# A two-bank score tile and another placement of PSUM banks in the attention stage, and a per-tile end of the down product, in a hybrid decoder block on Trainium2

## The chip, the cores and the metric

The kernel runs on one core of one Trainium2 chip. The metric is device time in microseconds (us), the median of several runs. The profile is one further execution, recorded by the hardware profiler. Engines are named as the profile names them: PE is TensorE (PEld its weight loads), DVE VectorE, ACT ScalarE, POOL GpSimd, SP the queue that issues most DMAs. PSUM, which matmuls write to, is used by this kernel as 8 banks of 512 float32 columns.

## The reference

One decoder block over 1024 tokens of 1024 channels, in float32. The input weight gives a pool branch, queries, keys, values and gates; the attention has 8 query heads on 2 key-value heads of 64 channels, in blocks of 128 queries that see their own and the previous 128 keys, with one sink logit for each head. The MLP is a squared ReLU of width 4096.

```python
def _rmsnorm(x, g):
    xf = x.astype(jnp.float32)
    r = lax.rsqrt(jnp.mean(xf * xf, axis=-1, keepdims=True) + EPS)
    return (xf * r * g.astype(jnp.float32)).astype(x.dtype)
...
    h = _rmsnorm(x, g_mix_pre[l])
    proj = jnp.einsum('bsd,de->bse', h, w_in[l]) + b_in[l]
    u_pool, q, k, v, gates = jnp.split(proj, IN_SPLITS, axis=-1)
...
    y_pool = _multiscale_pool(u_pool, w_pool[l], pool_scale[l])
    q = _partial_rotary(q.reshape(B, S, N_Q_HEADS, HEAD_DIM), cos, sin)
    k = _partial_rotary(k.reshape(B, S, N_KV_HEADS, HEAD_DIM), cos, sin)
...
    y_attn = _sliding_window_sink_attention(
        q.reshape(B, S, N_KV_HEADS, GROUP, HEAD_DIM), k, v, attn_sinks[l])
...
    merged = (g_pool * jnp.einsum('bsc,cd->bsd', y_pool, w_branch_pool[l])
              + g_attn * jnp.einsum('bsc,cd->bsd', y_attn, w_branch_attn[l]))
    mix = jnp.einsum('bsd,de->bse', merged, w_out[l])
    x = x + _rmsnorm(mix, g_mix_post[l])
    h2 = _rmsnorm(x, g_mlp_pre[l])
    ff = jnp.einsum('bsf,fd->bsd',
                    jnp.square(jax.nn.relu(jnp.einsum('bsd,df->bsf', h2, w_up[l]))), w_down[l])
    x = x + _rmsnorm(ff, g_mlp_post[l])
```

## The kernel before

Every float32 operand is split into a high part (a cast on ACT) and the rest (a subtraction on DVE), by `split` (L98, L99), and each product is made of three passes (`PASSES`): high by high, high by low, low by high. One matmul of 512 columns starts about 0.23 us after the one before it. The program is written once in its logical order; a scheduler then orders the instructions of each engine, by readiness and by the tile buffers that are free, and each engine runs its own list strictly in order.

The stages follow one another on TensorE: queries, keys and values of the first four tiles of 128 tokens (the loop over `k` from L162, with `mm_q` L147 and `mm_kv` L153); the attention stage, where the remaining four tiles' products (`qkv_tile`) and later the pool branch's input products (`pool_u`, through `mm_fm`, L345 and L347) are put between the attention's own short matmuls; the pool mixing (`pool_mix`, L524); the gates, the branch products, the output product and the up and down products of the MLP. Gates, up and down go by Strassen's seven products over two-by-two blocks (class `Pairs`, matmuls at L408, for gates and up; L1015 for down).

In the attention stage `post_qkv(n)` transposes queries and keys of tile n into two PSUM banks (L239, L240) and splits them. `score(n, g)` forms the scores of four heads of a tile, 128 queries by 256 keys each. Heads come in pairs, one on each key-value head; the two halves of 64 channels lie on partitions 0 to 63 and 64 to 127 of the same operands, and each half writes a bank of its own. For each of 16 groups (n, g) twelve matmuls (L268) fill two banks, four DVE reductions (L275) add the mask, scale, copy the scores to SBUF and give the row maxima. `attend(n, g)` follows: exponentials with their sums on ACT (L287, L290), the denominator (L292, L293) and the multiplication (L294) on DVE, eight transposes (L300), their splits, twelve matmuls with the values (L307) and a copy (L310). Tile 0 has only its own 128 keys.

The PSUM pool `ps` has two rings of four banks, "at" and "mm". In the attention stage "at" serves the transposed queries and keys, the scores (two banks each time), the transposed weights and the attention's outputs; "mm" serves the query, key and value products and `pool_u`.

`mean_sq` (L706) gives one root mean square for `out_post` and `out_norm`: two Squares with sums on ACT, an addition on DVE, then `rsqrt` (L101): a square root on ACT and five short DVE operations, one of them a Newton step.

The down product runs seven block products of 8 steps each, 24 matmuls for each step, in the order 1, 5, 2, 3, 6, 7, 4. Operands are loaded two steps ahead (`operands`), the blocks of the down weight stay in SBUF in 24 slots of the pool `rp`. The last product (4) ends in tile order: its last `LATE` steps are done for tile after tile, 6 matmuls for each step and tile. Then come the addition to the accumulated block (L1079), the Square and the gain (`fin_half`, L1021, L1022), and `finish` (L1026 on): the sum of the two halves, `rsqrt`, a load of the residual row (L1030), two fused multiply-adds (L1033) and two output transfers. For the last product these are called as

```python
for n0, n1 in ((), ((4, 6),), ((6, 7),), ((7, 8),))[t]:
    finish(n0, n1, (u, v))
```

Of the kernel before, what the change touches and what calls it, by code (L numbers as in the profile page):

```python
# [50 lines left out]
def block_kernel(ctx: ExitStack, tc, xt, x, consts, vecs, sinks, b_qkv, g_post, g_mlp, g_mlp_post,  # L51
# [9 lines left out]
    ps = ctx.enter_context(tc.tile_pool(name="ps", bufs=4, space=bass.MemoryType.PSUM))  # L61
# [23 lines left out]
    def bank(tag, shape=None):  # L85
        return ps.tile([P] + (shape or [512]), F32, tag=tag, name=nm(tag))
# [14 lines left out]
    def rsqrt(out_r, sums, n):  # L101
# [4 lines left out]
        dve.tensor_scalar(ms[:, :n], sums, 1.0 / D, EPS, ALU.mult, ALU.add)  # L106
        r = small()
# [49 lines left out]
    bq = {0: bank("at"), 1: bank("at"), 2: bank("mm"), 3: bank("mm")}  # L157
    bkv = {0: bank("at", [2, 256]), 2: bank("mm", [2, 256])}
# [75 lines left out]
    def post_qkv(n):  # L234
        tf = tfs.pop(n)
        t = tf[:, :768].rearrange("p (h d) -> p h d", d=HD)
        bt, bk = bank("at"), bank("at")
# [15 lines left out]
    def score(n, g):  # L253
# [8 lines left out]
        sb = [bank("at", [2, 256]) for _ in range(2)]  # L262
        for i in range(2):
            m = 2 * g + i
            for j, (qx, kx) in enumerate(((0, khi), (0, klo), (1, khi))):
                for kv in range(2):
                    r = slice(kv * HD, (kv + 1) * HD)
                    pe.matmul(sb[kv][:, i, :nk], qt[r, qx, m * P:(m + 1) * P], kx[r, k0:k0 + nk],  # L268
                              start=j == 0, stop=j == 2)

        for i in range(2):
            for kv in range(2):
                j = 2 * i + kv
                h = 4 * g + j
                dve.tensor_tensor_reduce(s4[:, j, :nk], sb[kv][:, i, :nk], msk, -HD ** -0.5, nsnk[:, h:h + 1],  # L275
# [205 lines left out]
    def pool_u(gi):  # L481
        whi, wlo = load_w(w_u[gi], [NK, P])
        bs = [bank("mm"), bank("mm")]
        mm_fm(bs, whi, wlo, xr, NK)
        u = ga_.tile([P, S], F32, tag="ga", name=nm("u"))
        for th in range(2):
            sl = slice(th * 512, (th + 1) * 512)
            dve.tensor_tensor(u[:, sl], bs[th], rb[:, sl], ALU.mult)
# [51 lines left out]
    ap_pool.__exit__(None, None, None)  # L540
    gp_pool = tc.tile_pool(name="gp", bufs=17, reuse_waits="tile")
# [164 lines left out]
    def mean_sq(src_halves, junk_halves):  # L706
        a = small(2, "sq")
        for i in range(2):
            act.activation(junk_halves[i], src_halves[i], AF.Square, accum_out=a[:, i:i + 1])
        dve.tensor_tensor(a[:, 0:1], a[:, 0:1], a[:, 1:2], ALU.add)  # L710
        r = small(1, "rr")
        rsqrt(r, a[:, 0:1], 1)
# [250 lines left out]
    res = {}  # L963
# [54 lines left out]

    def fin_half(n, dj, v):

        act.activation(junk, v, AF.Square, accum_out=sq[:, dj, n:n + 1])  # L1021
        dve.tensor_tensor(v, v, gfin_b[:, dj * 512:(dj + 1) * 512], ALU.mult)  # L1022
# [22 lines left out]
    for j, (i, s_) in enumerate(steps):  # L1045
# [37 lines left out]
        if i == 6:  # L1083
            finish(0, 4, (c11, c12))
# [71 lines left out]
```

## Time and profile before

| | before |
|---|---|
| median of 3 runs | 1163.75 us (1163.31 to 1164.55) |
| the profiled execution | 1163.43 us |
| its span, first to last instruction | 1161.6 us |
| mean granted TensorE clock | 0.996 |
| last value product of attention (L307) starts | 172.63 |
| last of the pool branch's input products (L347) starts | 195.1 |
| last output on VectorE (L1033) ends | 1158.01 |

Times inside the profile count from the start of the span. A matmul's busy time is from its start to its modelled end, and successive ones overlap, so rates are read from starts. "PE at L268 x12" in the chain of waits is a stretch of twelve instructions of TensorE on tiles of the ring "at" from line 268.

### The profile page before, as it was taken

What the parts mean: (1) busy time and instruction counts of PE and PEld (TensorE: products, weight loads), DVE (VectorE), ACT (ScalarE), POOL (GpSimd) and SP (SyncE); (2) the same over time, 40 slices, a digit from 0 to 9 for tenths busy, and PEclk for the clock granted to TensorE, in tenths of its full rate; (3) what the DMA queues carried; (4) which work ended last, traced back from release to release, by engine and by line L of the source; (5) the groups of instructions that cost most, each with busy time, mean ns of one, the idle gap of its engine ahead of it and who ended that gap; (6) DMA issues with size and microseconds to landing.
All of it is one profiled execution on the core that took longest, in us unless ns stands there. A gap on an engine that the chain in (4) does not pass through costs nothing.

```text
span 1161.6 us, 14370 instructions
## 1 busy us (share of the span) xinstructions
PE 1137.1 (98%) x5356; PEld 941.3 (81%) x5356; DVE 827.4 (71%) x1337; ACT 533.8 (46%) x926; POOL 53.5 (5%) x66
## 2 busy tenths in 40 slices
PE   7999999999999999999999999999999999999995
PEld 6888888788888887888788888888888888888884
DVE  7767899888754585777998766667558945447795
ACT  6445655653332233464655453535344345344341
POOL 3411100000000050000000000000000000000000
PEclk9999999999999999999999999999999999999998
DMA  7202114545245453333266434353788564332852
GB/s 257 66 1 91 38 55 163 200 172 172 110 174 189 145 199 109 127 128 127 91 217 217 171 128 181 118 181 118 285 294 295 202 194 133 91 104 77 273 181 91
DMA packets 66167, 179.11 MB, mean 154 GB/s; under 512 B 6192, under 2 KB 6192, under 8 KB 66096
## 3 DMA queue, kind: packets, MB, share of 16 engines
q1 hardware_dynamic: 60480, 157.99, 40.3%
q10 hardware_dynamic: 5616, 20.19, 4.5%
q8 instruction: 42, 0.69, 0.3%
q14 instruction: 29, 0.24, 0.1%
HBM read 127.82 MB, written 50.33 MB: 153 GB/s over the span
## 4 chain that ended last, share of the span: by engine, by line
PE 91%; DVE 4%; ACT 2%; DMA 2%; issue 1%; SPq 0%; DVEq 0%; ACTq 0%
PE mm L408 21%; PE at L408 16%; PE at L1015 15%; PE mm L1015 11%; PE mm L345 8%; PE mm L732 5%; PE mm L347 4%; PE mm L147 3%; PE at L307 2%; PE at L268 2%; PE mm L153 1%; PE at L147 1%; PE at L300 1%; DMA st<-in_w_up_dram 1%; DVE T L99 1%
## 5 line engine op out<-in xcount | busy, mean ns | idle before, releaser
L1015 PE MATMUL at<-ar,wh 128*128 128x512 f32 x744 | 169.3, 389 | 0.0
L1015 PEld LDWEIGHTS at<-ar,wh 128*128 128x128 f32 x744 | 139.6, 188 | 29.0
L1015 PE MATMUL mm<-ar,wh 128*128 128x512 f32 x576 | 131.0, 389 | 0.0
L99 DVE TENSOR_TENSOR wh<-raw,wh 128x1024 fp32r<-128x1024 f32 x53 | 64.8, 1224 | 86.4 <-ACT wh L98 86.4
L1015 PEld LDWEIGHTS mm<-ar,wh 128*128 128x128 f32 x576 | 108.1, 188 | 22.5
L98 ACT CAST wh<-st 128x512 fp32r<-128x512 f32 (+1 forms) x106 | 67.0, 641 | 119.6 <-PE mm L408 36.9
L98 ACT CAST wh<-raw 128x1024 fp32r<-128x1024 f32 x53 | 55.8, 1053 | 134.5 <-PE at L1015 63.4
L99 DVE TENSOR_TENSOR wh<-st,wh 128x512 fp32r<-128x512 f32 (+1 forms) x106 | 82.9, 790 | 18.3 <-ACT wh L98 16.1
L408 PE MATMUL mm<-gr,wh 128*128 128x512 f32 x300 | 72.4, 391 | 0.1
L408 PE MATMUL mm<-T,wx 128*128 128x512 f32 x288 | 67.6, 389 | 0.0
L408 PEld LDWEIGHTS mm<-gr,wh 128*128 128x128 f32 x300 | 56.0, 188 | 12.0 <-ACT g L797 0.5
L408 PEld LDWEIGHTS mm<-T,wx 128*128 128x128 f32 x288 | 54.1, 188 | 11.2
L408 PE MATMUL at<-T,wx 128*128 128x512 f32 x252 | 59.1, 389 | 0.0
L408 PEld LDWEIGHTS at<-T,wx 128*128 128x128 f32 x252 | 47.3, 188 | 9.8
L408 PE MATMUL mm<-x,wh 128*128 128x512 f32 x216 | 51.5, 390 | 0.9 <-ACT g L415 0.9
L99 DVE TENSOR_TENSOR ar<-B,ar 128x1024 fp32r<-128x1024 f32 x37 | 45.1, 1220 | 7.3 <-ACT ar L98 7.3
L408 PEld LDWEIGHTS mm<-x,wh 128*128 128x128 f32 x216 | 40.4, 188 | 10.1 <-ACT g L415 1.7
L408 PE MATMUL at<-gr,wh 128*128 128x512 f32 x183 | 44.6, 390 | 0.0
L290 ACT ACTIVATE s<-s,nmx 128x256 f32<-128x256 f32 (+1 forms) x64 | 31.3, 493 | 26.5 <-DVE nmx L275 26.4
L98 ACT CAST ar<-B 128x1024 fp32r<-128x1024 f32 x37 | 38.9, 1050 | 9.0 <-DMA B<-in_w_dn_dram 4.7
L408 PEld LDWEIGHTS at<-gr,wh 128*128 128x128 f32 x183 | 34.3, 188 | 7.6 <-DVE wh L99 0.4
L650 DVE TENSOR_TENSOR g<-g,mm 128x512 f32<-128x512 f32 x32 | 20.6, 683 | 27.7 <-PE mm L347 27.6
(332 smaller groups left out, 2292.8 us busy)
## 6 DMA issues: line engine op xcount, KB each, us to landing
raw<-f_dram SPq DMA_DIRECT2D x53, 512.0 KB, 3.7
f_dram<-g SPq DMA_DIRECT2D x30, 512.0 KB, 3.3
B<-in_w_dn_dram SPq DMA_DIRECT2D x24, 512.0 KB, 6.3
st<-in_w_up_dram SPq DMA_DIRECT2D x22, 512.0 KB, 3.7
f_dram<-g ACTq DMA_DIRECT2D x17, 512.0 KB, 2.6
st<-in_w_g_dram SPq DMA_DIRECT2D x16, 512.0 KB, 3.7
g<-spill_dram SPq DMA_DIRECT2D x16, 512.0 KB, 4.4
raw<-in_w_dn_dram SPq DMA_DIRECT2D x16, 512.0 KB, 4.6
```

The source lines that it names most:

```text
L98: act.copy(hi, src)
L99: eng.tensor_tensor(lo, src, f32(hi), ALU.subtract)
L147: pe.matmul(bq, xs_[k][n // 4][:, xh, n % 4 * P:(n % 4 + 1) * P], wq[k][:, h, :], start=k == 0 and j == 0, stop=k == NK - 1 and j == 2)
L268: pe.matmul(sb[kv][:, i, :nk], qt[r, qx, m * P:(m + 1) * P], kx[r, k0:k0 + nk], start=j == 0, stop=j == 2)
L290: act.activation(s4[:, j, :nk], s4[:, j, :nk], AF.Exp, scale=-1.0, bias=nmx[:, h:h + 1], accum_out=den[:, h:h + 1])
L307: pe.matmul(yb.rearrange("p m q -> p (m q)"), vs[k0 // P + kb][:, vh, kv * HD:kv * HD + P], pts[kv][:, ph, kb, :], start=j == 0, stop=j == ...
L345: pe.matmul(bs[th], whi[:, k, :], rhs(k, hl, th), start=k == 0 and hl == 0, stop=False)
L347: pe.matmul(bs[th], wlo[:, k, :], rhs(k, 0, th), start=False, stop=k == nk - 1)
L408: pe.matmul(b, w[:, wh, kt, :], xo[kt][:, xh, :], start=not after and kt == 0 and j == 0, stop=kt == 3 and j == 2, skip_group_check=after)
L650: dve.tensor_tensor(z[:, sl], z[:, sl], bs[th], ALU.mult)
L732: pe.matmul(obs[n][dj], l, wos[k][whl][:, dj * 512:(dj + 1) * 512], start=k == 0 and hl == 0 and whl == 0, stop=k == NK - 1 and hl == 1)
L1015: pe.matmul(bs[t], fo[fh][:, k2, t * P:(t + 1) * P], wo_[wh][:, k2, :], start=not after and s2 == 0 and k2 == 0 and j == 0, stop=s2 == NS ...
```

## The change

In the attention stage a pool `psa` replaces `ps`: one tile "sc" of two banks, and rings of three banks "at" and "mm". Both halves of a score group go into the one "sc" tile, so they get their banks together; their matmuls have high priority, and the order of the passes is changed. The first query products use the "sc" tile and "mm", the first key and value products "at". `post_qkv` takes its banks from "mm" for tiles 2 to 7. `pool_u` makes its two halves of 512 tokens one after the other, each with a bank of its own. After `pool_in(0)` the old `ps` with its two rings of four is opened, with waits by tile.

`mean_sq` and the end use a new `rsqrt_sum`: the Squares are scaled by D to the power of -1/2, epsilon is added to one of the two sums ahead of time, and the square root takes the other sum with that as its bias.

In the down product `LATE` is 3; each tile of the last product is finished by itself, its gained half goes into the accumulator `c11`, which is free by then, the residual rows of tiles 4 to 7 are loaded in front into slots of `rp`, the half that is ready earlier (`dj` 1) goes out first, and the last tile's transfer of that half is issued by ACT.

```diff
@@ -58,7 +58,9 @@
     sp = ctx.enter_context(tc.tile_pool(name="sp", bufs=3))
-    ps = ctx.enter_context(tc.tile_pool(name="ps", bufs=4, space=bass.MemoryType.PSUM))
+    psa_pool = tc.tile_pool(name="psa", bufs=1, space=bass.MemoryType.PSUM)
+    psum = {"pool": psa_pool.__enter__(), "bufs": {"sc": 1, "at": 3, "mm": 3}}
@@ -83,7 +85,7 @@
     def bank(tag, shape=None):
-        return ps.tile([P] + (shape or [512]), F32, tag=tag, name=nm(tag))
+        return psum["pool"].tile([P] + (shape or [512]), F32, tag=tag, name=nm(tag), bufs=psum["bufs"][tag])
@@ -115,6 +117,29 @@
+    ROOT_D = D ** -0.5
+    def rsqrt_sum(out_r, a, b, n=1):
+        s = small()
+        ms = small()
+        if n == 1:
+            act.activation(s[:, :1], a, AF.Sqrt, bias=b)
+            dve.tensor_tensor(ms[:, :1], a, b, ALU.add)
+        else:
+            dve.tensor_tensor(ms[:, :n], a, b, ALU.add)
+            act.activation(s[:, :n], ms[:, :n], AF.Sqrt)
+        r = small()
+        dve.reciprocal(r[:, :n], s[:, :n])
+        t = small()
+        if n == 1:
+            dve.scalar_tensor_tensor(t[:, :1], r[:, :1], r[:, :1], ms[:, :1], ALU.mult, ALU.mult)
+        else:
+            dve.tensor_tensor(t[:, :n], r[:, :n], r[:, :n], ALU.mult)
+            dve.tensor_tensor(t[:, :n], t[:, :n], ms[:, :n], ALU.mult)
+        dve.tensor_scalar(t[:, :n], t[:, :n], -0.5, 1.5, ALU.mult, ALU.add)
+        dve.tensor_tensor(out_r, r[:, :n], t[:, :n], ALU.mult)
@@ -154,8 +179,9 @@
-    bq = {0: bank("at"), 1: bank("at"), 2: bank("mm"), 3: bank("mm")}
-    bkv = {0: bank("at", [2, 256]), 2: bank("mm", [2, 256])}
+    bq01 = bank("sc", [2, 512])
+    bq = {0: bq01[:, 0, :], 1: bq01[:, 1, :], 2: bank("mm"), 3: bank("mm")}
+    bkv = {0: bank("at", [2, 256]), 2: bank("at", [2, 256])}
     bss = bank("at", [NT])
@@ -234,7 +260,7 @@
         t = tf[:, :768].rearrange("p (h d) -> p h d", d=HD)
-        bt, bk = bank("at"), bank("at")
+        bt, bk = (bank("at" if n < 2 else "mm") for _ in range(2))
         for m in range(4):
@@ -259,20 +285,22 @@
         nmx = soft[n][0]
-        sb = [bank("at", [2, 256]) for _ in range(2)]
-        for i in range(2):
-            m = 2 * g + i
-            for j, (qx, kx) in enumerate(((0, khi), (0, klo), (1, khi))):
-                for kv in range(2):
-                    r = slice(kv * HD, (kv + 1) * HD)
-                    pe.matmul(sb[kv][:, i, :nk], qt[r, qx, m * P:(m + 1) * P], kx[r, k0:k0 + nk],
-                              start=j == 0, stop=j == 2)
+        sb = bank("sc", [2, 2, 256])
+        with tc.high_priority():
+            for i in range(2):
+                m = 2 * g + i
+                for j, (qx, kx) in enumerate(((0, klo), (1, khi), (0, khi))):
+                    for kv in range(2):
+                        r = slice(kv * HD, (kv + 1) * HD)
+                        pe.matmul(sb[:, kv, i, :nk], qt[r, qx, m * P:(m + 1) * P], kx[r, k0:k0 + nk],
+                                  start=j == 0, stop=j == 2)
...
                 h = 4 * g + j
-                dve.tensor_tensor_reduce(s4[:, j, :nk], sb[kv][:, i, :nk], msk, -HD ** -0.5, nsnk[:, h:h + 1],
+                dve.tensor_tensor_reduce(s4[:, j, :nk], sb[:, kv, i, :nk], msk, -HD ** -0.5, nsnk[:, h:h + 1],
                                          ALU.add, ALU.min, nmx[:, h:h + 1])
@@ -480,12 +508,15 @@
         whi, wlo = load_w(w_u[gi], [NK, P])
-        bs = [bank("mm"), bank("mm")]
-        mm_fm(bs, whi, wlo, xr, NK)
         u = ga_.tile([P, S], F32, tag="ga", name=nm("u"))
...
             sl = slice(th * 512, (th + 1) * 512)
-            dve.tensor_tensor(u[:, sl], bs[th], rb[:, sl], ALU.mult)
+            b = bank("mm")
+            for k in range(NK):
+                for j, (xh, h) in enumerate(PASSES):
+                    pe.matmul(b, (whi, wlo)[h][:, k, :], xr(k, xh, th), start=k == 0 and j == 0,
+                              stop=k == NK - 1 and j == 2)
+            dve.tensor_tensor(u[:, sl], b, rb[:, sl], ALU.mult)
         act.activation(u, u, AF.Identity, bias=vec[:, V_BU + gi:V_BU + gi + 1])
@@ -538,6 +569,10 @@
     ap_pool.__exit__(None, None, None)
+    psa_pool.__exit__(None, None, None)
+    psum["pool"] = ctx.enter_context(tc.tile_pool(name="ps", bufs=4, space=bass.MemoryType.PSUM,
+                                                reuse_waits="tile"))
+    psum["bufs"] = {"at": 4, "mm": 4}
     gp_pool = tc.tile_pool(name="gp", bufs=17, reuse_waits="tile")
@@ -706,10 +741,11 @@
         for i in range(2):
-            act.activation(junk_halves[i], src_halves[i], AF.Square, accum_out=a[:, i:i + 1])
-        dve.tensor_tensor(a[:, 0:1], a[:, 0:1], a[:, 1:2], ALU.add)
+            act.activation(junk_halves[i], src_halves[i], AF.Square, scale=ROOT_D, accum_out=a[:, i:i + 1])
+        b = small()[:, :1]
+        dve.tensor_scalar(b, a[:, 0:1], EPS, None, ALU.add)
         r = small(1, "rr")
-        rsqrt(r, a[:, 0:1], 1)
+        rsqrt_sum(r, a[:, 1:2], b)
         return r
@@ -960,7 +996,7 @@
     junk = dl.tile([P, 512], F32, tag="junk", name="junk", bufs=1)
-    res = {}
+    res, xf = {}, {}
@@ -1016,25 +1052,37 @@
+    def fin_sq(n, dj, v):
+        act.activation(junk, v, AF.Square, scale=ROOT_D, accum_out=sq[:, dj, n:n + 1])
+    def fin_gain(dj, o, v):
+        dve.tensor_tensor(o, v, gfin_b[:, dj * 512:(dj + 1) * 512], ALU.mult)
     def fin_half(n, dj, v):
-        act.activation(junk, v, AF.Square, accum_out=sq[:, dj, n:n + 1])
-        dve.tensor_tensor(v, v, gfin_b[:, dj * 512:(dj + 1) * 512], ALU.mult)
-    def finish(n0, n1, hv):
-        ns = slice(n0, n1)
-        dve.tensor_tensor(sq[:, 0, ns], sq[:, 0, ns], sq[:, 1, ns], ALU.add)
-        rsqrt(rr[:, ns], sq[:, 0, ns], n1 - n0)
-        for n in range(n0, n1):
-            xs = stage([D])
-            nc.sync.dma_start(xs, x1_dram[n])
-            for dj in range(2):
-                o = xs[:, dj * 512:(dj + 1) * 512]
-                dve.scalar_tensor_tensor(o, hv[dj][n % 4], rr[:, n:n + 1], o, ALU.mult, ALU.add)
-                nc.sync.dma_start(out[n][:, dj * 512:(dj + 1) * 512], o)
+        fin_sq(n, dj, v)
+        fin_gain(dj, v, v)
+    def load_x1(n):
+        t = rp.tile([P, 2, 512], F32, tag="w", name=nm("xf"))
+        nc.sync.dma_start(flat(t), x1_dram[n])
+        xf[n] = t
+    def add_eps(ns, dj):
+        dve.tensor_scalar(sq[:, dj, ns], sq[:, dj, ns], EPS, None, ALU.add)
+    def fin_out(n, hv):
+        if n not in xf:
+            t = stage([2, 512])
+            nc.sync.dma_start(flat(t), x1_dram[n])
+            xf[n] = t
+        for dj in (1, 0):
+            o = xf[n][:, dj, :]
+            dve.scalar_tensor_tensor(o, hv[dj][n % 4], rr[:, n:n + 1], o, ALU.mult, ALU.add)
+            (nc.scalar if dj and n == NT - 1 else nc.sync).dma_start(out[n][:, dj * 512:(dj + 1) * 512], o)
     PRODUCTS = (1, 5, 2, 3, 6, 7, 4)
-    LATE = 2
+    LATE = 3
     steps = [(i, s_) for i in PRODUCTS for s_ in range(NS)]
@@ -1075,13 +1123,22 @@
             else:
+                n = 4 + t
                 down_mm(i, s_, bs, False, [(s2, k2, t) for s2 in range(NS - LATE, NS) for k2 in range(2)])
                 dve.tensor_tensor(u[t], u[t], bs[t], ALU.add)
-                fin_half(4 + t, 0, u[t])
-                for n0, n1 in ((), ((4, 6),), ((6, 7),), ((7, 8),))[t]:
-                    finish(n0, n1, (u, v))
+                fin_sq(n, 0, u[t])
+                fin_gain(0, c11[t], u[t])
+                rsqrt_sum(rr[:, n:n + 1], sq[:, 0, n:n + 1], sq[:, 1, n:n + 1])
+                fin_out(n, (c11, v))
+        if i == 7:
+            add_eps(slice(4, NT), 1)
+            for n in range(4, NT):
+                load_x1(n)
         if i == 6:
-            finish(0, 4, (c11, c12))
+            add_eps(slice(0, 4), 1)
+            rsqrt_sum(rr[:, 0:4], sq[:, 0, 0:4], sq[:, 1, 0:4], 4)
+            for n in range(4):
+                fin_out(n, (c11, c12))
     rpool.__exit__(None, None, None)
```

## The prediction

> **What bounds the kernel now.** I read the summary of busy time first, then a table of stretches (start:end, length, busy time and instructions of TensorE, its weight loads, VectorE, ScalarE and GpSimd).
>
> ```profile
> span 1161.6 us, 14370 instructions
> ...
> PE 1137.1 (98%) x5356; PEld 941.3 (81%) x5356; DVE 827.4 (71%) x1337; ACT 533.8 (46%) x926; POOL 53.5 (5%) x66
> ...
> 60.00:108.00 48.00, 48.00 (x332) 41.45 (x332) 31.67 (x86) 24.62 (x75) 8.81 (x15) 1.00 0.08 26
> 108.00:140.00 32.00, 31.52 (x220) 25.98 (x217) 26.41 (x82) 20.74 (x70) 3.83 (x9) 1.00 0.24 79
> 140.00:173.00 33.00, 32.84 (x202) 27.33 (x201) 30.43 (x74) 19.49 (x53) 0.00 (x0) 1.00 0.14 49
> 173.00:196.00 23.00, 23.00 (x106) 19.16 (x105) 21.27 (x36) 11.21 (x16) 0.00 (x0) 1.00 0.45 160
> 196.00:229.00 33.00, 31.89 (x138) 25.43 (x137) 28.17 (x45) 22.31 (x37) 0.00 (x0) 1.00 0.54 184
> ...
> 500.00:545.00 45.00, 44.83 (x205) 36.53 (x204) 31.96 (x78) 24.43 (x64) 0.00 (x0) 1.00 0.41 142
> ```
>
> TensorE works 98% of the span and its clock is full (the 1.00 before the DMA share), so an edit pays only if it takes matmul time away, fills a pause of TensorE, or shortens the end, where TensorE is done. But a busy TensorE is not one at its best rate. In the attention stage the chain of waits (start, length, what) shows the same score work at two prices:
>
> ```profile
> 59.72 0.78 PE at L268 x5
> 61.79 0.78 PE at L268 x6
> ...
> 107.72 0.91 PE at L268 x12
> 108.63 1.02 PE at L300 x8
> ...
> 125.29 0.91 PE at L268 x6
> 126.19 1.50 PE at L307 x11
> 127.69 0.90 PE at L268 x6
> ...
> 145.38 1.32 PE at L307 x11
> ...
> 159.44 0.91 PE at L268 x6
> ...
> 163.01 0.90 PE at L268 x6
> ...
> 172.63 1.30 PE at L307 x11
> ...
> 228.80 1.36 PE at L408 x6
> ```
>
> Twelve score matmuls with the two key-value halves in turn take 0.91 us (107.72): the halves lie on different rows of the array and run side by side. Six of one half alone take 0.91 us too (125.29), and the other six follow later (127.69). This chain shows 8 of the 14 groups of tiles 1 to 7 split so, from 59.72/61.79 to 159.44/163.01: the second half's bank was not free in time, so the order of before puts other work between.
>
> **The change part by part.**
>
> *Scores.* In the order of the changed kernel all 14 groups stand as twelve neighbours with the halves alternating, since both get their banks at once. Eight times 0.90 us: −7.2 us.
>
> *The wait that it adds.* There is one such pair of banks. A group's scores wait until the four reductions (L275) of the group before have read it; behind them on TensorE, which runs in order, wait the transposes, value products and fillers. And the products of the pool branch (L345, L347) have lost their place: the banks of the last tiles' transposes (L239) now come from the ring that the pool branch needs, so only 32 of its 192 matmuls stand inside the attention stage; before, the first stood at 109.4:
>
> ```profile
> L345 PE MATMUL mm<-x,wh x128: 387/389/504, 109.4 to 194.6; 128*128 128x512 f32 x128
> ...
> L347 PE MATMUL mm<-x,wh x64: 387/389/504, 114.0 to 195.1; 128*128 128x512 f32 x64
> ```
>
> So after the last QKV product comes a stretch with 10 groups to be transposed and multiplied with the values, but hardly a filler. Before gets there at 107.72 with 8 score groups left, after with 6. Its start of that stretch: three of the split groups lie ahead of it (−2.7), two score groups more are done (+1.8), and the stage begins worse (+1.7), as the timeline of its start suggests:
>
> ```profile
> 53.28 1.28 ACT L290 ACT_TABLE_LOAD   x1 [0.80 <-DVE nmx L275]
> ...
> 56.35 0.17 DVE L292 TENSOR_TENSOR den<-den,es 128x4 f32<-128x4 f32 x1 [0.98 <-ACT s L290]
> ```
>
> The first exponentials wait for a table load of 1.28 us, and L292 waits for them. The order of after puts this L292 ahead of the reductions that free the pair for the next scores; the 1.7 is an estimate, the load and 0.4 for what queues behind it. 107.72 + 0.8 = 108.5. VectorE's prices, from its timeline further on:
>
> ```profile
> 108.66 0.48 DVE L275 CUSTOM_DVE_ANT_0 s<-at,cst,nsnk 128x256 f32<-128x256 f32 x1
> ...
> 109.88 0.48 DVE L275 CUSTOM_DVE_ANT_0 s<-at,cst,nsnk 128x256 f32<-128x256 f32 x1
> ...
> 110.29 1.29 DVE L99 TENSOR_TENSOR pt<-at,pt 128x512 fp32r<-128x512 f32 x2
> 111.50 0.15 DVE L286 TENSOR_TENSOR es<-snk,nmx 128x4 f32<-128x4 f32 x1
> ...
> 123.50 0.18 DVE L293 RECIPROCAL den<-den 128x4 f32<-128x4 f32 x1
> 123.71 1.22 DVE L294 TENSOR_TENSOR s<-s,den 128x1024 f32<-128x1024 f32 x1
> 124.88 1.29 DVE L99 TENSOR_TENSOR pt<-at,pt 128x512 fp32r<-128x512 f32 x2
> ```
>
> Four reductions take 1.63 us (108.66 to 110.29), the multiplication 1.17 (123.71 to 124.88), the two splits 1.21 (110.29 to 111.50), the three short ones about 0.15 each. Ten groups: 10 × 2.83 + 6 × 1.63 = 38.1 us, and the splits of two tiles' queries and keys, by the row of two splits some 0.8 a tile, 1.6 more: 39.7. TensorE has 10 × (1.02 + 1.32) + 6 × 0.91 + 32 × 0.23 + twelve transposes of these tiles, 1.5 by the row of eight = 37.7. The two are near each other and VectorE is the longer, so the stretch ends near 108.5 + 41 = 149.5, with 1.3 us for hops between engines. The 160 pool matmuls left follow at the rate of the last block (24.64 us for 108, quoted below): 36.5 us, to 186.0. Before, the last of them started at 195.1 and ended its share at 195.3. That is 9.3 us ahead.
>
> *What it gives back.* After the pool branch its split must again come ahead of L524 and of the gate's first products. With the pool work in one block TensorE can wait some 2 us there, where 1.1 stand idle now (196 to 229: 31.89 of 33), so 9.3 − 1 = 8.3 is left. That supposes each engine always has its next instruction ready. In the order of after, a multiplication (L294) often stands among the reductions that free the pair, so some groups come later: I take −7.0. Ends: −9.6, if the hops cost nothing; and if each of the six remaining groups waits for a multiplication (6 × 1.17) and VectorE also carries two splits of pool weights in the stretch, 2.4 us by the same rate, 8.3 − 7.0 − 2.4 = −1.1, a loss of about 1 us.
>
> [...]
>
> *Mean squares.* Epsilon is added beside the second Square and the root is taken right behind it, so one handover from VectorE to ScalarE goes and the count on VectorE stays. The stretch from 500 to 545, where most of them are, has TensorE busy for 44.83 of 45: hidden. −0.2, between 0 and −0.8.
>
> *The end.* Three rather than two steps of the last product are done tile by tile, each tile is finished by itself, and the residual rows are in place beforehand.
>
> ```profile
> 1124.80 24.64 PE L1015 MATMUL at<-ar,wh 128*128 128x512 f32 x108
> ...
> 1132.97 1.05 ACT L98 CAST wh<-raw 128x1024 fp32r<-128x1024 f32 x1 [3.44 <-PE at L1015]
> ...
> 1151.15 0.69 DVE L1022 TENSOR_TENSOR u<-u,bc 128x512 f32<-128x512 f32 x1
> ...
> 1151.83 0.68 DVE L1079 TENSOR_TENSOR u<-u,at 128x512 f32<-128x512 f32 x1
> ...
> 1153.14 0.19 ACT L1021 ACTIVATION_READ_ACCUMULATOR junk<-u 128x1 f32 x1
> ...
> 1155.44 0.29 ACT L104 ACTIVATE sm<-fsq,eps 128x1 f32<-128x1 f32 x1 [2.11 <-DVE fsq L1026]
> ...
> 1155.77 0.16 DVE L108 RECIPROCAL sm<-sm 128x1 f32<-128x1 f32 x1 [0.17 <-ACT sm L104]
> ...
> 1156.60 0.75 DVE L1033 SCALAR_TENSOR_TENSOR st<-u,frr,st 128x512 f32<-128x512 f32 x1
> 1157.27 0.74 DVE L1033 SCALAR_TENSOR_TENSOR st<-v,frr,st 128x512 f32<-128x512 f32 x1
> ```
>
> The last matmul ends at 1124.80 + 24.64 = 1149.44, the last tile's addition starts only at 1151.83, because VectorE is still finishing tiles 4 to 6. The root waits until 1155.44, though its sum is there at 1153.33, behind two outputs and the gain of tiles 6 and 7. After the change a tile costs: addition to sum 1.50 (1151.83 to 1153.33), root 0.35 with its hop, reciprocal to the first output 0.83 (1155.77 to 1156.60), two outputs 0.67 + 0.74: 4.1 us, and VectorE can take the next tile 4.03 after the one before. TensorE delivers the tiles 16, 18 and 18 matmuls apart, 11.86 us by 24.64/108 each, against 3 × 4.03 = 12.09: the last tile starts about 0.2 late. The third late step needs the last operand sooner: its slot comes free at 1132.97 and the operand, two casts and VectorE's splits, is ready about 3.45 us later, while 15 matmuls, 3.41 us, stand ahead of its use: under 0.1 us. So the last output ends at 1149.44 + 0.1 + 0.25 + 4.1 = 1153.9, where it ended at 1158.01: −4.1, and the final transfer, 3.6 us to the end of the span, stays behind it. I take −4.0. Ends: −4.4; and −2.9, if each of the four tiles loses 0.3 us in hops. The residual's loads are issued in product 3 on SP between loads that wait for the same splits, so nothing is held up by them.
>
> *Sum,* in the profiled execution's own time of 1163.43 us (span 1161.6 and 1.8 around it): 1163.43 − 7.0 − 0.2 − 4.0 = 1152.2; the median of the runs shown, 1163.75, is 0.3 above it, so 1152.5.
>
> **The rivals.**
>
> 1. *The pair of banks is the limit.* TensorE's gain in the scores turns whole into waits for the reductions; the stretch of ten groups lasts as long as its fillers did. For it: VectorE's 39.7 us against TensorE's 37.7, and 30.43 of 33 busy on VectorE already. Against it: the fillers' time is not lost, it is done later at full rate. Attention 0 to −2, end and mean squares −4.2: 1163.75 − 5.2 = 1158.5.
>
> 2. *Slower.* The pair comes free late by a multiplication, 1.17 us, for each of the 14 groups, and nothing fills the pause: 16.4 us, with the start's 1.7, against 7.2 + 4.2 gained: +6.7, 1170; it decides from (11.4 − 1.7)/14 = 0.7 us per group on. For it: TensorE runs in order and there is one pair. Against: in the first half the order has QKV products between the groups, and VectorE is busy for 31.67 of 48 there, so only the six late groups have no cover: −11.4 + 1.7 + 6 × 1.17 is still a gain.
>
> 3. *The end does not shorten as told:* the outputs of the last tiles come close together and the final transfer lasts longer, or the late operand stops TensorE by more than 1 us. For it: the slot of 1132.97 is on the edge. Against: the outputs of before were as dense. End 0, the rest −7.2: 1156.5.
>
> 4. *More than forecast:* the sum above holds without the margin, −8.3 to −9.6, with −4.4 and −0.8: 1163.75 − 13.5 to − 14.8, about 1149.5.
>
> **How the numbers follow.** Forecast 0.50, the fourth case 0.13, the first 0.20, the third 0.06, the second 0.11. About 0.2% is what a measurement of this kernel can tell from no change. The range reaches from 1148, under the fourth case with a margin of 1 us, to 1160.5, past the first and third; outside lie the second case and the edges. Slower 0.09, since the second case can also end near no change, same 0.03, faster 0.88. The forecast's own range is 1149.5 to 1156.
>
> **What would show it.** In the profile after: all score groups as runs of twelve in 0.91 us; L345 and L347 mostly after the last value product, which ends near 149, not 174; the first matmul of L408 into "at" near 221, not 228.8; the stage of the up product of equal length; the last tile's addition within 0.5 us of the last matmul, and 12.2 us from that matmul to the end of the span turned into about 8. It is wrong if TensorE shows pauses of a microsecond at most score groups, if the value products still end after 160, or if the last addition still starts 2 us late.

## The result, and the profile after

The changed kernel takes 1156.03 us (median of 4 runs, 1155.0 to 1157.23) against 1163.53 us (4 runs, 1163.2 to 1164.55): a ratio of 0.9933, with a 95% interval of 0.992 to 0.9946. That is 7.5 us less, where 11.3 less was forecast. The profiled execution took 1155.82 us, with a span of 1154.0.

Summary of busy time of the kernel after:

```profile
span 1154.0 us, 14409 instructions
...
PE 1131.8 (98%) x5356; PEld 937.4 (81%) x5356; DVE 826.6 (72%) x1339; ACT 535.0 (46%) x927; POOL 49.1 (4%) x66
```

Its table of stretches, with the columns of the prediction's:

```profile
60.00:108.00 48.00, 47.05 (x326) 39.19 (x324) 36.30 (x118) 28.07 (x97) 6.05 (x16) 0.96 0.01 2
108.00:140.00 32.00, 30.91 (x249) 26.62 (x250) 30.08 (x87) 24.95 (x79) 3.03 (x8) 1.00 0.34 116
...
196.00:229.00 33.00, 31.41 (x136) 24.72 (x135) 27.15 (x43) 18.61 (x32) 0.00 (x0) 1.00 0.49 172
```

TensorE's busy time fell by 5.3 us (1137.1 to 1131.8), the span by 7.6. Two stretches have lost something: from 60 to 108 TensorE stands idle for 0.95 us, where it had no idle time, and its clock is 0.96; and from 108 to 140 VectorE is busy for 30.08 of 32.

The scores do what the diff says. From the chain of waits after (start, length, what):

```profile
100.84 0.91 PE sc L296 x12
...
154.15 19.96 PE mm L517 x88
```

All groups now stand as one run of about 0.9 us, and the products of the pool branch (L517), but for the first 32, follow the last values as one block. To see where the time came from, milestones are better than shares. These are groups of instructions of the kernel after (count: shortest, median and longest duration in ns, first and last start in us, shape):

```profile
L178 PE MATMUL mm<-wkv,x x96: 274/283/562, 50.5 to 111.5; 128*128 128x256 f32 x96
L335 PE MATMUL at<-pt,v x180: 274/282/415, 61.3 to 153.9; 128*128 128x256 f32 x180
L517 PE MATMUL mm<-x,wh x192: 389/389/482, 127.9 to 191.4; 128*128 128x512 f32 x192
L768 PE MATMUL mm<-wohi,gr x128: 389/389/482, 442.3 to 530.8; 128*128 128x512 f32 x128
L1051 PE MATMUL at<-gr,wh x24: 389/389/389, 841.5 to 846.7; 128*128 128x512 f32 x24
```

and of the kernel before:

```profile
L153 PE MATMUL mm<-wkv,x x144: 277/283/384, 12.8 to 107.4; 128*128 128x256 f32 x144
L307 PE MATMUL at<-pt,v x180: 274/282/388, 59.4 to 173.6; 128*128 128x256 f32 x180
L732 PE MATMUL mm<-wohi,gr x128: 389/389/476, 445.7 to 533.9; 128*128 128x512 f32 x128
L1015 PE MATMUL at<-gr,wh x24: 389/389/389, 844.6 to 849.8; 128*128 128x512 f32 x24
```

The last key and value product starts 4.1 us later than before (111.5 against 107.4), but with three more score groups done. The score matmuls ahead of that point, first before, then after (start:end, length, busy time and instructions of TensorE and of its weight loads):

```profile
50.00:107.50 57.50, 9.46 (x84) 7.34 (x84) 1.00 0.06 18
...
50.00:111.50 61.50, 9.58 (x120) 7.68 (x120) 0.97 0.02 7
```

At twelve for a group these are seven groups and ten. The last value product starts 19.7 earlier, since the pool products now come behind it; the last of those starts 3.7 earlier (191.4 against the 195.1 of L347), and the output product 3.4 earlier, the down product 3.1. So the attention stage gave 3.4 us, where 7.0 were forecast, and 0.3 was lost again between output and down product.

The end, from the timeline of the kernel after (start, length, engine, line, operation):

```profile
1123.68 22.88 PE L1051 MATMUL at<-ar,wh 128*128 128x512 f32 x99
...
1142.73 0.68 DVE L1128 TENSOR_TENSOR u<-u,at 128x512 f32<-128x512 f32 x1
...
1146.70 0.68 DVE L1128 TENSOR_TENSOR u<-u,at 128x512 f32<-128x512 f32 x1
...
1150.00 0.74 DVE L1081 SCALAR_TENSOR_TENSOR xf<-c,frr,xf 128x512 f32<-128x512 f32 x1
```

The last matmul ends at 1123.68 + 22.88 = 1146.56, and the last tile's addition starts 0.14 us later, where it was 2.39 late before. A tile takes VectorE 3.97 us (1142.73 to 1146.70). From the last matmul to the end of the span are 7.4 us instead of 12.2, so the end gave 4.7.

The start of the attention stage cost more than was forecast. First VectorE and then TensorE, from the timeline around it:

```profile
57.09 0.16 DVE L320 TENSOR_TENSOR den<-den,es 128x4 f32<-128x4 f32 x1 [1.93 <-ACT s L318]
...
57.38 0.32 DVE L303 CUSTOM_DVE_ANT_0 s<-sc,cst,nsnk 128x128 f32<-128x128 f32 x1
...
58.68 0.39 PE L296 MATMUL sc<-klo,qt 64*128 64x256 f32 x2 [2.13 <-DVE nmx L303]
```

The table of stretches there:

```profile
56.00:58.00 2.00, 0.55 (x6) 0.31 (x3) 0.87 (x7) 1.25 (x7) 0.00 (x0) 1.00 0.00 0
...
60.00:62.00 2.00, 1.87 (x8) 1.38 (x6) 2.00 (x6) 1.38 (x6) 1.36 (x4) 0.50 0.00 0
62.00:64.00 2.00, 2.00 (x10) 1.82 (x9) 2.00 (x11) 0.38 (x2) 0.00 (x0) 0.65 0.00 0
```

L320 waits 1.93 us for the first exponentials, the four reductions that empty the pair of banks stand behind it on VectorE, and the third group's scores stand behind those: TensorE pauses for 2.13 us. Then its granted clock falls to 0.50 from about 60 on (0.65 over 62 to 64), and the matmuls of that time count as busy while they take twice as long: the key and value product at 60.02 takes 0.56 us, where the median of its group is 0.283. Busy time alone would not have shown it; the clock column does.

### The profile page after: what moved, and what is told of

The parts are those of the page before. It is cut to its first block, busy times and chain, and to the rows that moved or that the text cites. A ratio compares the mean times of both kernels' runs of the same rounds, so it can differ in the third digit from the quotient of the medians.

```text
span 1154.0 us, 14409 instructions
## 1 busy us (share of the span) xinstructions
PE 1131.8 (98%) x5356; PEld 937.4 (81%) x5356; DVE 826.6 (72%) x1339; ACT 535.0 (46%) x927; POOL 49.1 (4%) x66
## 4 chain that ended last, share of the span: by engine, by line
PE 88%; DVE 5%; ACT 4%; DMA 2%; issue 1%; SPq 0%; DVEq 0%; ACTq 0%
PE mm L436 20%; PE at L436 16%; PE at L1051 14%; PE mm L1051 11%; PE mm L768 5%; PE mm L373 5%; PE mm L517 4%; PE mm L172 3%; PE mm L375 2%; PE at L335 2%; PE sc L172 1%; PE at L178 1%; PE sc L296 1%; ACT s L318 1%; PE at L328 1%
## 5 line engine op out<-in xcount | busy, mean ns | idle before, releaser
L436 PE MATMUL mm<-x,wh 128*128 128x512 f32 x216 | 51.4, 391 | 0.5 <-ACT g L443 0.5
L436 PEld LDWEIGHTS mm<-x,wh 128*128 128x128 f32 x216 | 40.3, 188 | 9.7 <-ACT g L443 1.1
L517 PE MATMUL mm<-x,wh 128*128 128x512 f32 x192 | 47.7, 393 | 0.0
L517 PEld LDWEIGHTS mm<-x,wh 128*128 128x128 f32 x192 | 35.4, 188 | 6.5
```

Source lines behind the costliest of these rows:

```text
L436: pe.matmul(b, w[:, wh, kt, :], xo[kt][:, xh, :], start=not after and kt == 0 and j == 0, stop=kt == 3 and j == 2, skip_group_check=after)
L517: pe.matmul(b, (whi, wlo)[h][:, k, :], xr(k, xh, th), start=k == 0 and j == 0, stop=k == NK - 1 and j == 2)
```

## The experiments

Each kernel ran beside the kernel before on the same chip. Each expectation says what the theories it weighs would give.

| Kernel | Median, us | Ratio to before | 95% interval |
|---|---|---|---|
| after | 1156.03 | 0.9933 | 0.992 to 0.9946 |
| end_only | 1160.33 | 0.9962 | 0.995 to 0.9974 |
| late2 | 1156.71 | 0.9934 | 0.9922 to 0.9946 |
| exp_early | 1154.12 | 0.9907 | 0.9893 to 0.992 |
| red_first | 1157.94 | 0.9943 | 0.9932 to 0.9954 |
| score_serial | 1154.77 | 0.9919 | 0.9905 to 0.9933 |
| score_twice | 1170.9 | 1.0065 | 1.0053 to 1.0078 |
| post_at | 1153.08 | 0.9908 | 0.9894 to 0.9922 |
| post_at_exp | 1159.12 | 0.9963 | 0.995 to 0.9976 |
| post_at47_exp | 1157.58 | 0.9947 | 0.9933 to 0.9961 |
| post_at_exp_yt | 1152.45 | 0.9913 | 0.9899 to 0.9926 |
| post_at_yt | 1155.74 | 0.9935 | 0.9922 to 0.9947 |
| best_wide | 1152.48 | 0.9901 | 0.9884 to 0.9919 |

**end_only: the end and the mean squares alone.** The kernel before, with only `rsqrt_sum`, `mean_sq` and the new end of the diff.

```diff
-        rsqrt(r, a[:, 0:1], 1)
+        rsqrt_sum(r, a[:, 1:2], b)
...
-    LATE = 2
+    LATE = 3
```

> The kernel before with only the new end and the new mean square; the attention stage is that of before. By the two traces the last matmul ends 2.9 us earlier after the change and the way from there to the end of the span is 4.7 us shorter (12.16 to 7.45), so theory A (the parts are independent) expects about 1163.5 - 4.7 - 0.2 = 1158.6 us. Theory B (part of the 2.9 us comes from the mean squares in the middle) expects under 1157.5.

By the ratio it is 4.4 us faster than before (0.0038 of 1163.5), which leaves 0.9962 − 0.9933 = 0.0029, or 3.4 us, for the attention part; both ratios are good to about 1.4 us. The traces of after divide it in a like way: 3.4 up to the output product and 4.7 at the end, with 0.5 lost between them. The mean squares lie between the output product and the down product, and there is nothing in it, by groups of this kernel:

```profile
L756 PE MATMUL mm<-wohi,gr x128: 389/389/476, 447.1 to 535.4; 128*128 128x512 f32 x128
...
L1039 PE MATMUL at<-gr,wh x24: 389/389/390, 846.1 to 851.3; 128*128 128x512 f32 x24
```

From the first start of one to the first of the other are 399.0 us, before 398.9.

**late2: two instead of three late steps.**

```diff
-    LATE = 3
+    LATE = 2
```

> The changed kernel with two rather than three steps of the last product in tile order. Theory A: TensorE then delivers a tile each 2.7 us and VectorE takes 4.0 for one, so the last tile starts about 3 x 1.3 = 3.9 us late instead of 0.2, less what the sooner operand saves: 1159 to 1160. Theory B: the finish tile by tile is the whole gain: within 0.5 us of 1156.

The medians can't tell it from after. Its profile can. Timeline:

```profile
1124.73 21.24 PE L1051 MATMUL at<-ar,wh 128*128 128x512 f32 x93
...
1146.79 0.67 DVE L1128 TENSOR_TENSOR u<-u,at 128x512 f32<-128x512 f32 x1
...
1151.38 0.74 DVE L1081 SCALAR_TENSOR_TENSOR xf<-c,frr,xf 128x512 f32<-128x512 f32 x1
```

The last matmul ends at 1145.97, the last addition starts 0.82 later, and the last output ends at 1152.12, 6.15 behind the last matmul; after, it was 1150.74 − 1146.56 = 4.2. So the third late step is worth 2 us behind the last matmul in this execution, less than was expected: VectorE interleaves two tiles here (the third tile's addition starts at 1143.37, between two short operations of the second tile, at 1143.29 and 1143.96), and the 4.0 us that one tile takes in after include waits for ACT (0.17 us ahead of L133) that the next tile's work can fill.

**exp_early: the exponentials' table loaded ahead of the stage.** One small exponential more, behind the root of the input sums.

```diff
     rsqrt(r1, bss[:, :NT], NT)
+    act.activation(warm, r1[:, :1], AF.Exp)
```

> The changed kernel with one exponential of a spare value put behind the first square root, so that the table load of 1.28 us falls before the attention stage. Theory A: the missing gain is lost at the start, where the pair of banks is read late behind the table load, TensorE pauses 2.1 us at 56 and then runs at half clock from 60 to 63.5; without the load the pause shrinks under 1 us, no half clock follows: 2 to 3 us less, 1153 to 1154. Theory B: the loss is spread over all groups by the single pair of banks: at most 1 us less, 1155 to 1156.

It is 0.0026, or 3.0 us, better than after by the ratios and 1.9 by the medians; the two intervals only touch. Its table of stretches:

```profile
56.00:58.00 2.00, 1.08 (x11) 0.84 (x10) 1.27 (x6) 0.63 (x5) 0.00 (x0) 1.00 0.00 0
...
60.00:62.00 2.00, 2.00 (x20) 1.86 (x18) 1.66 (x8) 1.37 (x6) 1.65 (x4) 1.00 0.00 0
```

Its key and value products, by groups:

```profile
L178 PE MATMUL mm<-wkv,x x96: 277/283/385, 51.5 to 109.8; 128*128 128x256 f32 x96
```

The pause has shrunk to 0.92 us, the half clock at 60 is gone, and the longest of the products takes 385 ns, not 562. From the first to the last of them are 58.3 us instead of 61.0, so the start cost after 2.7 us. All that this kernel gains is there: from the last of them to the output product are 330.7 us, after 330.8. In this execution it gives back 1.0 us ahead of the stage: the first of these products starts at 51.5, in after at 50.5, behind a half clock from 44 to 48 (0.51, then 0.63) that the trace of after does not have (1.00).

**red_first: the reductions ahead.** The loop of the four reductions stands in `tc.high_priority()`.

```diff
+        with tc.high_priority():
             for i in range(2):
                 for kv in range(2):
```

> The changed kernel with the four reductions of each group at high priority like their matmuls, so that they stand ahead of denominators and multiplications on VectorE and free the pair sooner. Theory A (loss at the start): the reductions of the second group no longer wait for the first exponentials, the pause at 56 goes: 2 to 3 us less, 1153 to 1154. Theory B (the pair is the limit in every group): still more, 3 to 5 us less. Theory C (VectorE's total is the limit): earlier reductions only delay the multiplications: within 1 us of 1156.

It is about 1 us slower than after by the ratios, which the intervals leave open; it is not faster. At the start it did not do what it was for: the denominator still comes first and the pause stays. Later on, the value products wait longer for the casts of the weights. Waits of TensorE from 44 to 210 (engine, what, waited for: us in total, times, longest), first of this kernel, then of after:

```profile
PEld at L336 <- ACT pt L100: 4.7, 14, 0.5
...
PE sc L296 <- DVE nmx L304: 2.1, 1, 2.1
```

```profile
PEld at L335 <- ACT pt L100: 3.0, 9, 0.5
...
PE sc L296 <- DVE nmx L303: 2.1, 1, 2.1
```

In after, the matmuls of the scores wait for the reductions once for more than 0.2 us, the 2.1 us of the start. Past the start, then, the time at which the pair comes free isn't what binds. The waits for the casts grow from 3.0 to 4.7, those for the subtractions fall from 2.8 to 2.2; that the precedence of the reductions is the reason is not shown. This run does not test the start itself.

**score_serial: one half's three matmuls, then the other's.**

```diff
-                for j, (qx, kx) in enumerate(((0, klo), (1, khi), (0, khi))):
-                    for kv in range(2):
-                        r = slice(kv * HD, (kv + 1) * HD)
+                for kv in range(2):
+                    r = slice(kv * HD, (kv + 1) * HD)
+                    for j, (qx, kx) in enumerate(((0, klo), (1, khi), (0, khi))):
```

> The changed kernel with the twelve matmuls of a score group in another order: three of one half, then three of the other, twice, in the same two banks. A group takes then at least 1.4 us by the row of six of one half in 0.91, less up to three overlaps at the changes of half, instead of 0.91. Theory A (score time is on the path, as the forecast supposed): 14 groups x 0.5 to 0.9 = 7 to 12 us more, 1163 to 1168. Theory B (TensorE would only wait longer for VectorE and ScalarE in this stage, so the score time saved turned into waits): 0 to 3 us more, 1156 to 1159.

The time is that of after within the intervals. The order on TensorE is now low, high, high for one half and then the same for the other, but its timeline shows one group so:

```profile
139.76 0.39 PE L296 MATMUL sc<-klo,qt 64*128 64x256 f32 x2
...
139.99 0.41 PE L296 MATMUL sc<-khi,qt 64*128 64x256 f32 x4
```

Both low products of a head pair come first, then four high ones: the second half's first matmul starts beside the first half's, ahead of two that stand before it in the program. So the edit did not take the pairing away, and the run is a second sample of after. What it adds is that these halves need only be neighbours, not alternate: the group takes 0.92 us to the start of the next transpose (139.76 to 140.68), in after 0.90 (139.55 to 140.45).

**score_twice: every score matmul twice.** The group's twelve are repeated into the same banks.

```diff
+            for _ in range(2):
                 for i in range(2):
                     m = 2 * g + i
```

> The changed kernel with the twelve matmuls of each score group made twice in a row (the second dozen starts the same banks anew). This adds 0.91 us of TensorE work in each of the 14 groups of tiles 1 to 7 and 0.8 in the two of tile 0, 14.3 us. Theory A (matmul time of the scores is on the path): 12 to 14 us more than the changed kernel, 1168 to 1170. Theory B (in this stage TensorE mostly waits, so the 7.2 us that the pairing saved turned partly into waits): 3 to 8 us more, 1159 to 1164; if nearly all is hidden, under 3.

It is 14.9 us slower than after (1170.9 − 1156.03). Summary of this kernel:

```profile
span 1169.1 us, 14788 instructions
...
PE 1143.1 (98%) x5548; PEld 949.3 (81%) x5548; DVE 829.2 (71%) x1339; ACT 535.3 (46%) x927; POOL 49.4 (4%) x66
```

TensorE is busy for 11.3 us more and idle for 3.8 more. The doubling was priced at 14.3, so time added to the scores is on the path in full. A saving there should then be a saving of the kernel, unless something new is lost beside it. By itself the run does not tell whether the pair of banks is the limit, since a chain of scores and reductions would grow with the scores as well; that is read from the waits shown under red_first.

**post_at: the transposes' banks from "at" for all tiles,** so that the ring "mm" has room for the pool products inside the stage.

```diff
-        bt, bk = (bank("at" if n < 2 else "mm") for _ in range(2))
+        bt, bk = (bank("at") for _ in range(2))
```

> The changed kernel with the transposes of queries and keys back in the ring "at" for all tiles, so that the pool branch can start earlier: 74 instead of 32 of its 192 matmuls stand ahead of the last value product. Theory A (the missing filler makes the waits for casts and splits before the value products, 5.8 us of TensorE's weight loads in the trace after): 2 to 4 us less, 1152 to 1154. Theory B (three banks in that ring are too few for one more user): the same or slower, 1156 to 1159.

1153.08, some 2.9 us better than after by the ratios, with intervals that just overlap. But the earlier pool products are not what gains. Groups of this kernel:

```profile
L178 PE MATMUL mm<-wkv,x x96: 277/283/387, 51.3 to 109.5; 128*128 128x256 f32 x96
...
L517 PE MATMUL mm<-x,wh x192: 387/389/497, 110.4 to 189.9; 128*128 128x512 f32 x192
```

The pool products do start earlier, 110.4 instead of 127.9. Yet from the last key and value product to the last pool product are 80.4 us, after 79.9: where the fillers stand is worth nothing. The gain is again in the first part, 58.2 us instead of 61.0. So the median lies in the range of theory A, but not for its reason.

**post_at_exp and post_at47_exp: both edits,** in the second with "at" for tiles 0, 1 and 4 to 7 (`"at" if n < 2 or n > 3 else "mm"`).

> Both: the transposes in "at" and the early exponential of exp_early. If the two losses (start and filler) are separate, the gains add: 1156 - 2 - 3 = 1151; if the filler brings nothing, 1154 as exp_early.

> As post_at_exp, but the transposes of tiles 2 and 3 stay in "mm" and only those of tiles 4 to 7 go to "at"; 79 pool matmuls stand ahead of the last value product. If the filler is what counts, as post_at_exp within 1 us; if the ring "at" is too tight early on, up to 2 us faster than it.

Neither adds up; they are slower than either edit alone. Of post_at_exp, a piece of the chain of waits:

```profile
194.44 7.18 DMA spill_dram<-u
```

its waits from 190 to 215:

```profile
ACT ar L100 <- DMA spill_dram<-u: 4.3, 1, 4.3
...
PE at L556 <- ACT ar L100: 3.4, 1, 3.4
```

and its table of stretches:

```profile
206.00:210.00 4.00, 4.00 (x10) 3.09 (x10) 0.15 (x1) 3.39 (x5) 0.00 (x0) 0.50 0.77 287
```

The mixing's result goes out of the slot of `u` (`yt = us.pop(gi)`), and the next split takes a slot of that ring. The transfer takes 7.18 us, where it took 3.89 in after (`194.98 3.89 DMA spill_dram<-u` in its chain); TensorE waits 3.4 us and then has half the clock (0.50 from 206 to 210). The second kernel loses at the same place (a transfer of 7.27, a wait of 3.8, clock 0.72 from 200 to 206).

**post_at_exp_yt and post_at_yt: the mixing's result in another ring,** with the early exponential and without.

```diff
-        yt = us.pop(gi)
+        us.pop(gi)
+        yt = flat(yy.tile([P, 2, 512], F32, tag="y", name=nm("yt")))
```

> post_at_exp with the pooled output in a tile of another pool, so that the split of the next pooled group no longer waits for a slot that a transfer to HBM still reads. Theory A: that transfer (7.2 us in post_at_exp), the pause of 3.4 us behind it and the half clock after the pause are what cost post_at_exp 6 us against post_at: without them 1150 to 1152. Theory B: the stall moves to another wait at the same place: 1155 or more.

> The same tile of another pool in post_at alone. If the transfer costs only where it comes late, as post_at within 1 us, 1152 to 1154; if it also holds post_at, up to 2 us less.

With the early exponential the wait is gone, and the median goes from 1159.12 to 1152.45. The stretch, of post_at_exp_yt:

```profile
196.00:229.00 33.00, 32.82 (x143) 26.20 (x143) 29.37 (x50) 17.50 (x29) 0.00 (x0) 1.00 0.55 190
```

TensorE is busy for 32.82 of 33 there, after 31.41. Without the early exponential the edit is no better than post_at alone: 1155.74 against 1153.08, outside both expected ranges. Its trace loses the time from 196 to 229, where TensorE is busy for 29.74 us (31.73 in post_at) and waits 1.8 us for a cast of the mixing's operand and 1.5 for ScalarE at the gates. Why these come late was not followed up.

**best_wide: the best of these, with the input sums 64 columns wide.** Four profiles (end_only, exp_early, post_at, post_at_exp) show a half clock from about 44 to 48 (0.50 to 0.73 in stretches of 2 us), right behind the sixteen one-column matmuls that sum the squares, and no pause of TensorE over 0.1 us before it. So the last kernel makes them wider, on top of post_at_exp_yt.

```diff
-        pe.matmul(bss[:, n:n + 1], sq[:, n * P:(n + 1) * P], ones, start=n == 0, stop=n == NT - 1)
+        pe.matmul(bss[:, n, :], sq[:, n * P:(n + 1) * P], ones.broadcast_to([P, 64]), start=n == 0, stop=n == NT - 1)
```

> post_at_exp_yt with the sixteen one-column matmuls of the sums of squares (at 42 to 44 us) made 64 columns wide. In the profiles so far TensorE ran at half clock either from 44 to 48 (end_only, exp_early, post_at, post_at_exp), or after the pause at 56 (all five with the start of the changed kernel), or not at all. Theory A: the thin stretch of one-column matmuls brings the first kind about; wider ones keep the array busy, no half clock stands in the profile, the runs lie closer together and the median is about 1 us lower, 1151 to 1152. Theory B: the width does not matter to the clock: 1152 to 1153, or up to 2 us slower if wider ones take longer.

1152.48 us (1152.3 to 1153.28 in 4 runs), no half clock in its profile (1.00 in every stretch from 40 to 229), and the runs lie closer together than those of post_at_exp_yt (1152.09 to 1154.65). Its interval (0.9884 to 0.9919) lies below that of after (0.992 to 0.9946), so it beats both kernels of the case, but exp_early, post_at and post_at_exp_yt can't be told from it. Whether the width keeps the clock up is not settled either: post_at_exp_yt and post_at_yt had no half clock there without it (1.00 from 44 to 48).

## Why the prediction was right and where it was wrong

The sign and the range were right, and so were the two main mechanisms, the joined scores and the end by tiles. The forecast was 3.5 us too low, and 1156.03 lies at the upper edge of its own range (1149.5 to 1156). The largest miss, 3.3 us, is in the start of one stretch; the smaller ones behind it and the margins nearly cancel.

- *Scores, −7.2.* Right in kind: the groups run as twelve in about 0.9 us, and ten of them take TensorE 9.58 us where seven took 9.46 (rows of the stretches 50 to 111.5 and 50 to 107.5). That time added to them is paid in full is shown by score_twice. The saving did not arrive whole because of the next point.
- *The start of the stretch, "107.72 + 0.8 = 108.5".* This step failed. The last key and value product ended at 111.5 + 0.28 = 111.8, 3.3 us later, and two of its three terms were too small. "Two score groups more are done (+1.8)" was a miscount: before had seven groups done there and nine left, not eight, and after has ten done, so there are three more. At 0.9 us for a group that accounts for 0.9. "The stage begins worse (+1.7)" named the right cause, the table load (1.28 us) and L292 (now L320) ahead of the reductions, but it cost 2.7 us (61.0 against 58.3 with exp_early), because the half clock that follows (0.50 from 60 to 62, 0.65 from 62 to 64) was not in the sum. That accounts for 1.0. Most of the 2.7 seems to be that half clock: post_at keeps the table load and pauses for 1.5 us, has no half clock behind it (1.00 from 60 to 64), and needs 58.2 too (post_at_yt likewise, 58.1). The other 1.4 have no term in the sum. Short waits may hold them. Waits of TensorE from 64 to 111, after:

```profile
PEld at L335 <- ACT pt L100: 1.6, 5, 0.4
PEld at L335 <- DVE pt L101: 1.6, 4, 0.5
PEld sc L296 <- DVE es L314: 0.7, 2, 0.4
PEld sc L296 <- issue: 0.6, 2, 0.4
PE at L335 <- DVE pt L101: 0.3, 1, 0.3
PEld sc L296 <- DVE nmx L303: 0.2, 1, 0.2
```

and before:

```profile
PEld at L307 <- ACT pt L98: 1.7, 5, 0.4
PEld at L268 <- issue: 0.7, 3, 0.3
```

They add up to 5.0 us after and to 2.4 before (4.2 in exp_early, so the start isn't what makes most of them). Most are waits of the weight loads, which overlap with matmuls that still run (TensorE itself is idle for 0.95 us from 60 to 108), so their difference of 2.6 is not time lost one for one. The two put down to L314 are no waits for the pair of banks, whose reductions had ended 0.5 us before. That the split scores of before had filled these gaps, six matmuls at a time, is a guess: score_serial was to part the halves again and did not.

- *The stretch and the block.* "41" measured 42.4 (111.8 to 154.2), and "36.5" for the pool products 37.6 (154.2 to 191.8), since the first mixing matmuls stand in that block too. The two prices of VectorE and TensorE were near enough; with the 3.3 above, these 2.5 us explain the 5.8 by which "186.0" was missed.
- *What it gives back.* From the last pool product's start to the output product before took 445.7 − 195.1 = 250.6 us, after 250.9: the 1 us allowed for the mixing was measured as 0.3, and the further 1.3 of margin was used up by the misses above.
- *Mean squares, −0.2.* Nothing: 399.0 us against 398.9 in end_only.
- *The end, −4.0.* Right: −4.7 in the traces, −4.4 by the ratio of end_only, which holds the mean squares too. The last addition is 0.14 us late where 0.2 was forecast, and a tile takes 3.97 us where 4.03 was. The late operand cost one wait of 0.4 us in the weight loads, where under 0.1 was allowed.
- *The rivals.* The pair of banks as the limit falls with the waits of after and with red_first, and the slower case with it: TensorE waits for the reductions for more than 0.2 us at one group, the third, not at fourteen. The end did shorten. The result lies near the number of the third rival, 1156.5, by chance and not for its reason. The fourth, more than forecast, did not come.

In this order of instructions the runs show one pair to be enough past the start (no wait for it over 0.2 us in after; red_first, no faster with the reductions ahead). At the start, where the reductions come late for another reason, it could have helped; a second pair was not tried.

## What to carry to other kernels

A saving on the busiest engine was predicted well; what is lost beside it was not. When a sum is taken at a milestone, count the groups done on each side from the trace: here one was missed, 0.9 us. Before a split group of short matmuls is joined, add up the short waits between the pieces as well; here 1.4 us had no term, and their cause stays open. And when a pause of a few microseconds is forecast, look at the clock column behind it: here the cost was the pause (2.13 us) and then a slower stretch (clock 0.50, then 0.65) that counts as busy.

## What the runs showed of the hardware

- *Half clock behind a short pause.* In all five profiles with the start of after (after, red_first, late2, score_serial, score_twice) TensorE's clock fell to about a half for some 3.5 us between 58 and 64, behind a pause of 1.7 to 2.1 us (2.13 in after). The lowest stretches of 2 us have 0.50, 0.55, 0.50, 0.53 and 0.50. Behind 1.5 us (post_at, post_at_yt) and 0.92 (exp_early) it did not fall (1.00 from 60 to 64).
- *Half clock without a pause.* In end_only TensorE is busy for all of 44 to 48, at a clock of 0.59:

```profile
44.00:48.00 4.00, 4.00 (x12) 3.19 (x12) 3.42 (x12) 0.56 (x2) 0.46 (x1) 0.59 0.00 0
```

What came just before are the sixteen one-column matmuls. Other profiles have the same sixteen and no half clock behind them (after: 1.00 from 44 to 48), so it does not come every time.
- *Row halves out of order.* In score_serial matmuls of the second half started ahead of two of the first half that come before them in the program (139.76 against 139.99). The section on the kernel before has each engine run its list strictly in order; here TensorE did not, since starts of the two halves' matmuls changed places.
- *One transfer, two lengths.* The same 512 KB out of `u` took 3.89 us in after and 7.18 in post_at_exp, while the DMA engines were busy for 0.68 and 0.93 of that time with it and other loads. So the price of this slot, which waits for a transfer, could not be taken from the other kernel's trace; that the traffic is the reason fits and was not tested by itself.
